# Encoder layer on one core: the feed-forwards in groups of four gate units, with seven block products in place of eight in two chunks of each eight

## The chip, the cores and the metric

The kernel runs on one core of one Trainium2 chip. The metric is device time in microseconds (us): 1980.3 us, the median of three runs of the kernel before (1979.99 to 1980.6).

## The reference, cut to what matters

One encoder layer over x[256, 2048] in float32. The two SwiGLU feed-forwards, which the change touches, hold most of the products; between them stands a mixer (one wide projection, a pooling branch, a convolution branch, an output projection).

```python
def rmsnorm(x, g):
    return x * rsqrt(mean(x * x) + EPS) * g
def swiglu(h, w_gate, w_up, w_down):          # w_gate, w_up: 2048 x 5632; w_down: 5632 x 2048
    return (silu(h @ w_gate) * (h @ w_up)) @ w_down

x = x + 0.5 * swiglu(rmsnorm(x, ffn1_norm), ffn1_w_gate, ffn1_w_up, ffn1_w_down)
x = x + mixer(rmsnorm(x, mix_norm))
x = x + 0.5 * swiglu(rmsnorm(x, ffn2_norm), ffn2_w_gate, ffn2_w_up, ffn2_w_down)
out = rmsnorm(x, final_norm)
```

## The kernel before, in words

**Products.** Every float32 operand is split into a high part (a cast to fp32r on ScalarE, ACT: `hi_lo`, line 135) and a low part (operand less high part on VectorE, DVE: line 137). A product is three matmuls: high by high, high by low, low by high (`products`, lines 203 to 214). The 256 tokens are two token tiles of 128; activations are the stationary operand (128 x 128), weights the moving one (128 x 512).

**The stream.** All weights pass through one stream of chunks. A chunk is two row tiles of 128 rows by 1024 columns, a tile of 512 KB each; a unit is all chunks of 1024 output columns. One ordinary chunk is 2 row tiles x 2 token tiles x 3 matmuls x 2 halves of 512 columns = 24 matmuls. A gate unit (512 columns of `w_gate` beside the same 512 of `w_up`) has 16 row tiles, so 8 chunks; each feed-forward has 11 gate units, then two down units (one for each half of the output) of 44 row tiles, so 22 chunks.

**The order.** It is written out by hand. For chunk i, `run` (lines 346 to 355) emits the loads of chunk i+2 on SP's queue, the split of chunk i+1 on ACT and DVE, then whatever `at` hung on chunk i, then the products of chunk i on TensorE (PE). Each engine goes through its own part in that order. Split tiles have four buffers for the high and four for the low parts (line 74), that is two chunks, so the split of a row tile of chunk i+1 waits until the matching row tile of chunk i-1 is used up; raw tiles have five buffers. In a unit's last chunk token tile 0 comes first, then token tile 1 (line 194).

**PSUM.** Accumulators are three buffers of two banks (line 77), so a unit starts while the last one is read out; two single banks serve transposes (line 78).

**After a gate unit** `gate_done` (lines 277 to 294) makes h = silu(gate) * up from the accumulators, for each token tile one ACT and one DVE instruction; two and three chunks later `put` turns h by PE transposes (line 250) and splits it into `ht`, which keeps all 11 units' hidden layer. The down units run after all gate units; `down_done` (lines 296 to 305) adds half their sum into the residual X and `squares` feeds the next norm. `next_operand` and `x_transposed` make the next transposed operand; for the first feed-forward `first_operand` makes it from `xT` during the first unit (lines 336 and 710).

Of the kernel before, what the change touches and what calls it, by code (L numbers as in the profile page):

```python
# [13 lines left out]
P = 128  # L14
# [21 lines left out]
# after these row tiles of weights, the row tiles of x^T that are loaded  # L36
# [4 lines left out]
# columns of the packed per-partition vectors  # L41
# [9 lines left out]
class Unit:  # L51
    """x[T, K*128] @ w[K*128, 1024]: K row tiles, two banks of 512 columns for each token tile."""

    def __init__(self, dram, k, lhs, done, tail=None):
        self.dram, self.k, self.lhs, self.done, self.tail = dram, k, lhs, done, tail
        self.acc = None


class Special:
    """A chunk of the weight stream with a use of its own."""  # L60
# [6 lines left out]
def encoder_kernel(ctx: ExitStack, tc: tile.TileContext, x, xT, vecs, rows, pool_m,  # L67
# [29 lines left out]
    def at(i, fn):  # L97
        """fn is emitted before the products of chunk i."""
        side.setdefault(i, []).append(fn)

    def amid(i, fn):
        """fn is emitted between the products of chunk i."""
        while isinstance(stream[i][0], Special):
            i += 1
        middle.setdefault(i, []).append(fn)

    class Pos:
        now = 0

# [10 lines left out]
    def load(i):  # L120
# [27 lines left out]
    def split_chunk(i, first=False):  # L148
# [3 lines left out]
        r = raw.pop(i)  # L152
        split[i] = []
# [11 lines left out]

    def bank(name):
        return ps_t.tile([P, C], F32, tag="T", name=name)

    def run_chunk(i):
# [33 lines left out]
    def products(u, k, t, w, cs=(0, 1)):  # L203
        xh, xl = u.lhs(k, t)
        wh, wl = w
        for n, (a, b) in enumerate(((xh, wh), (xh, wl), (xl, wh))):
            for c in cs:
# [4 lines left out]
                    start=k == 0 and n == 0,  # L212
                    stop=k == u.k - 1 and n == 2,
                )

    # ---------------------------------------------------------------- operands of the products
    def pair(pool, tag, n, name):
        """hi and lo by row tile, four row tiles to a block."""
# [9 lines left out]
    def hidden(pool, name):  # L228
        """The feed-forward's hidden layer, hi and lo by row tile, four of them in a block."""
        return [tuple(block(pool, f"h{s}{u}", F32R, f"{name}{s}{u}") for s in "hl") for u in range(FF // C)]  # L230
# [7 lines left out]
    def scaled_split(dst, src, gain):  # L238
        """dst = hi and lo of src * gain, a scalar of each partition."""
# [5 lines left out]
    def transposes(src_of, n, name):  # L245
        """n (up to 4 / NT) tiles [T, 128] into one bank as [128, T] each."""
        b = bank(name)
# [6 lines left out]
    def x_transposed(dst, gain_base, k0):  # L254
# [17 lines left out]
    # ---------------------------------------------------------------- feed-forward  # L272
    def ffn_units(w_g, w_d, xt, ht, rs, residual_done, tail=None):
        def hidden_lhs(k, t):
            return tuple(h[:, k % 4, t * P:(t + 1) * P] for h in ht[k // 4])

        def gate_done(u):
            def done(acc):
                hs = []
                for t in range(NT):  # L280
                    sg = stg.tile([P, C], F32, tag="sg", name=f"sg{Pos.now}_{t}")
                    h = stg.tile([P, C], F32, tag="h", name=f"h{Pos.now}_{t}")
# [4 lines left out]

                def put(k0):
                    b = transposes(lambda j, t: hs[t][:, (k0 + j) * P:(k0 + j + 1) * P], 2,
                                   f"hT{Pos.now}_{k0}")  # L290
                    hi_lo(b.rearrange("p (q t) -> p q t", q=2), *(h[:, k0:k0 + 2, :] for h in ht[u]))
                at(Pos.now + 2, lambda: put(0))
                at(Pos.now + 3, lambda: put(2))
            return done

        def down_done(half):
# [12 lines left out]
        for half in range(2):  # L309
# [517 lines left out]
```

## Time and profile before

| | before |
|---|---|
| runs | 1979.99, 1980.3, 1980.6 us |
| span of the profiled execution (first to last instruction) | 1978.6 us |
| instructions | 22916 |
| weights and other traffic read from HBM | 380.28 MB |

The profiled execution has no time of its own beside its span; the median of the runs lies 1.7 us above that span, which stands for what lies around it. PE is the matmuls, PEld the loads of the stationary operand that overlap them, DVE VectorE, ACT ScalarE, POOL GpSimd, SP the queue that issues the loads. The names in rows are those of the program: `acc` an accumulator, `wh` and `wl` the high and low weights, `xt1h` the high part of the first feed-forward's operand, `hT` the transposed hidden layer. A bracket behind a row gives the idle time before it and what ended it. Matmul durations overlap: the pace is read from their starts.

### The profile page before, as it was taken

The page shows a single profiled execution, that of the slowest core. Times are in us where ns is not written, and L with a number is a line of the kernel's source. Part 1 is how long each engine was busy: PE and PEld are TensorE (multiplying, and loading weights), DVE is VectorE, ACT ScalarE, POOL GpSimd, SP SyncE. Part 2 cuts the span into 40 slices and gives each one's busy share as a digit, 9 for nine tenths or more (in the row PEclk, how much of TensorE's full clock was granted, in tenths as well). Part 3 has the DMA queues.
Part 4 walks back from the last instruction along what each step waited for, and adds up shares of the span by engine and source line. Part 5 has one row for each costly group of instructions (what it writes and reads, how often), then busy time and mean ns, then how long its engine had stood idle before and what let it go on. Part 6 is the DMA issues. An engine that isn't in the chain of part 4 may idle for free.

```text
span 1978.6 us, 22916 instructions
## 1 busy us (share of the span) xinstructions
PE 1966.4 (99%) x8848; PEld 1629.5 (82%) x8848; DVE 1110.4 (56%) x1224; ACT 874.5 (44%) x997; POOL 11.0 (1%) x22
## 2 busy tenths in 40 slices
PE   9999999999999999999999999999999999999998
PEld 7888888888888888888888888888888888888886
DVE  5454544444445445888897765555544444444444
ACT  6444444444434345454444544544444444443433
POOL 0000000000000000000000000000000000000000
PEclk9999999999999999999999999999999999999999
DMA  8555555555555656666666555555555555565564
GB/s 310 193 188 196 190 192 188 187 189 190 192 191 187 195 189 202 194 195 211 202 208 205 184 185 185 181 186 198 191 188 189 189 190 192 181 198 195 192 192 149
DMA packets 106141, 383.88 MB, mean 194 GB/s; under 512 B 11920, under 2 KB 12176, under 8 KB 105776
## 3 DMA queue, kind: packets, MB, share of 16 engines
q1 hardware_dynamic: 104688, 378.45, 58.4%
q0 software_dynamic: 1056, 3.83, 0.6%
q8 instruction: 69, 1.13, 0.2%
q14 instruction: 40, 0.33, 0.1%
q10 hardware_dynamic: 288, 0.14, 0.0%
HBM read 380.28 MB, written 2.10 MB: 193 GB/s over the span
## 4 chain that ended last, share of the span: by engine, by line
PE 99%; DMA 1%; issue 0%; ACT 0%; DVE 0%; DVEq 0%; POOLq 0%; POOL 0%; ACTq 0%
PE acc L208 96%; PE hT L250 1%; PE xt L250 0%; DMA raw<-in_w_g 0%; PE mixb L560 0%; DMA xrh<-in_xT 0%; PE pool L535 0%; PE mT L250 0%; PE gT L250 0%; ACT fsq L668 0%; ACT wh L135 0%; PE ln_mean L442 0%; PE ln_var L471 0%; DVE X L680 0%; DVE X L665 0%
## 5 line engine op out<-in xcount | busy, mean ns | idle before, releaser
L137 DVE TENSOR_TENSOR wl<-raw,wh 128x1024 fp32r<-128x1024 f32 (+1 forms) x706 | 853.8, 1221 | 741.7 <-ACT wh L135 741.5
L135 ACT CAST wh<-raw 128x1024 fp32r<-128x1024 f32 (+1 forms) x706 | 736.2, 1050 | 906.9 <-PE acc L208 849.6
L208 PE MATMUL acc<-wh,xt1h 128*128 128x512 f32 x704 | 219.2, 392 | 1.8 <-ACT wh L135 0.9
L208 PE MATMUL acc<-wh,xt3h 128*128 128x512 f32 x704 | 218.9, 392 | 0.0
L208 PE MATMUL acc<-wl,xt1h 128*128 128x512 f32 x704 | 217.4, 390 | 0.1
L208 PE MATMUL acc<-wl,xt3h 128*128 128x512 f32 x704 | 217.1, 390 | 0.0
L208 PE MATMUL acc<-wh,xt1l 128*128 128x512 f32 x704 | 216.9, 389 | 0.0
L208 PE MATMUL acc<-wh,xt3l 128*128 128x512 f32 x704 | 216.8, 389 | 0.0
L208 PEld LDWEIGHTS acc<-wl,xt1h 128*128 128x128 f32 x704 | 132.1, 188 | 28.1 <-DVE wl L137 0.4
L208 PEld LDWEIGHTS acc<-wh,xt1l 128*128 128x128 f32 x704 | 132.1, 188 | 28.2 <-DVE xt1l L242 0.5
L208 PEld LDWEIGHTS acc<-wh,xt3l 128*128 128x128 f32 x704 | 132.1, 188 | 27.8
L208 PEld LDWEIGHTS acc<-wl,xt3h 128*128 128x128 f32 x704 | 132.1, 188 | 27.8
L208 PEld LDWEIGHTS acc<-wh,xt1h 128*128 128x128 f32 x704 | 130.6, 188 | 28.6 <-ACT wh L135 1.5
L208 PEld LDWEIGHTS acc<-wh,xt3h 128*128 128x128 f32 x704 | 130.5, 188 | 25.8
L208 PE MATMUL acc<-wh,xt2h 128*128 128x512 f32 x448 | 138.3, 390 | 0.0
L208 PE MATMUL acc<-wl,xt2h 128*128 128x512 f32 x448 | 138.1, 389 | 0.0
L208 PE MATMUL acc<-wh,xt2l 128*128 128x512 f32 x448 | 138.0, 389 | 0.0
L208 PE MATMUL acc<-wh,ht2h 128*128 128x512 f32 x352 | 109.2, 390 | 0.0
L208 PE MATMUL acc<-wl,ht2h 128*128 128x512 f32 x352 | 109.1, 389 | 0.0
L208 PE MATMUL acc<-wh,ht2l 128*128 128x512 f32 x352 | 109.0, 389 | 0.0
L208 PE MATMUL acc<-wh,ht1h 128*128 128x512 f32 x352 | 108.7, 390 | 0.0
L208 PE MATMUL acc<-wh,ht1l 128*128 128x512 f32 x352 | 108.4, 389 | 0.0
(144 smaller groups left out, 1699.9 us busy)
## 6 DMA issues: line engine op xcount, KB each, us to landing
raw<-in_w_g SPq DMA_DIRECT2D x350, 512.0 KB, 3.3
raw<-in_w_d SPq DMA_DIRECT2D x176, 512.0 KB, 3.5
raw<-in_w_in SPq DMA_DIRECT2D x112, 512.0 KB, 4.2
raw<-in_w_out SPq DMA_DIRECT2D x32, 512.0 KB, 4.2
raw<-in_w_pp SPq DMA_DIRECT2D x16, 512.0 KB, 4.0
raw<-in_w_cp SPq DMA_DIRECT2D x16, 512.0 KB, 4.0
row<-in_rows POOLq DMA_DIRECT2D x7, 512.0 KB, 4.2
X<-in_x SPq DMA_DIRECT2D x2, 1024.0 KB, 8.9
```

Source lines behind the costliest of these rows:

```text
L135: nc.scalar.copy(out=h, in_=src)
L137: nc.vector.tensor_tensor(out=l, in0=src, in1=h.bitcast(F32), op=ALU.subtract)
L208: nc.tensor.matmul(u.acc[t + c if u.tail and t else t][:, c, :], lhsT=a, rhs=b[:, c * C:(c + 1) * C], start=k == 0 and n == 0, stop=k == u ...
L250: nc.tensor.transpose(out=b[:, j * T + t * P: j * T + (t + 1) * P], in_=src_of(j, t), identity=ident)
```

## The change

- **Order.** The gate units come in groups of four: after gate units 0 to 4 come the two down units of the hidden rows of gate units 0 to 3 (8 chunks each), after gate units 5 to 8 those of gate units 4 to 7, after 9 and 10 those of the last three (6 chunks each). Each down unit adds into X; only the last two feed the norm. `ht` holds four gate units' hidden layer in place of eleven.
- **Seven products.** In chunks 0 and 3 of every gate unit but the first, and of the down units of the first two groups, the two row tiles and the two column halves of the weights, and the two row tiles and two token tiles of the activations, are taken as 2 x 2 blocks, and seven block products (Strassen's scheme in Winograd's form) replace eight. Three of them add into the unit's own accumulators, four into shared banks that serve several outputs.
- **Sums of weights.** `split_seven` makes four sums of 128 x 512 on DVE, one of them in place in the raw tile, and splits three more column blocks of 512 into high and low parts.
- **Differences of activations.** `e_forms` makes four of 128 x 128 on DVE and splits them: once a feed-forward for the operand's chunks 0 and 3 (`scaled_forms`), and for chunks 0 and 3 of every group's hidden layer in `put`, that is, for gate units 0, 4 and 8 in its first call and 1, 5 and 9 in its second.
- **Shared banks.** After chunk 3 `shared_parts` combines the four banks into two tiles in SBUF (one ACT copy, four DVE instructions). At the end the own accumulators are added to these (`gate_done_seven`), or both go into X one after the other (`into_residual`).
- **PSUM** is one tile of eight banks: four shared, four own, without a second set. `put` of a gate unit's hidden layer now runs in chunks 5 and 6 of the following gate unit, in two of the shared banks.

```diff
+GROUP = 4
+SEVEN = (0, 3)
+B_P1, B_P5, B_P6, B_P7, B_11, B_12, B_21, B_22 = range(8)
...
-    ps_a = ctx.enter_context(tc.tile_pool(name="ps_a", bufs=3, space=bass.MemoryType.PSUM))
-    ps_t = ctx.enter_context(tc.tile_pool(name="ps_t", bufs=2, space=bass.MemoryType.PSUM))
+    psp = ctx.enter_context(tc.tile_pool(name="psp", bufs=1, space=bass.MemoryType.PSUM))
+    ps = psp.tile([P, 8, C], F32, name="ps")
...
-                nc.sync.dma_start(out=r[:, s], in_=u.dram[2 * cc + kk, :, s])
+                nc.sync.dma_start(out=r[:, s], in_=u.dram[getattr(u, "k0", 0) + 2 * cc + kk, :, s])
...
+        if isinstance(u, Unit) and cc in u.seven:
+            split[i] = split_seven(i, *r)
+            return
...
+    def split_seven(i, r0, r1):
+        w11, w12, w21, w22 = r0[:, :C], r0[:, C:], r1[:, :C], r1[:, C:]
+        sm = ffn["pool"].tile([P, 3, C], F32, tag="sum", name=f"sum{i}")
+
+        def add(out, a, b):
+            nc.vector.tensor_tensor(out=out, in0=a, in1=b, op=ALU.add)
+        add(sm[:, 1, :], w12, w22)
+        add(w12, w11, w12)
+        add(sm[:, 0, :], w12, w22)
+        add(sm[:, 2, :], sm[:, 0, :], w21)
+        ext = tuple(ffn["pool"].tile([P, 3, C], F32R, tag=f"ext{x}", name=f"ext{x}{i}") for x in "hl")
+        return (hi_lo(r0, *stream_tiles(i, 0)), hi_lo(sm, *ext), hi_lo(r1, *stream_tiles(i, 1)))
...
     def bank(name):
-        return ps_t.tile([P, C], F32, tag="T", name=name)
+        Pos.bank += 1
+        return ps[:, 6 + Pos.bank % 2, :]
...
         if cc == 0:
             n = NT + 1 if u.tail else NT
-            u.acc = [ps_a.tile([P, 2, C], F32, tag="acc", name=f"acc{i}_{t}") for t in range(n)]
+            if u.seven:
+                u.acc = [ps[:, B_11:B_12 + 1, :], ps[:, B_21:B_22 + 1, :]]
+                Pos.acc = 0
+            else:
+                u.acc = [ps[:, 2 * ((Pos.acc + t) % 3):2 * ((Pos.acc + t) % 3) + 2, :] for t in range(n)]
+                Pos.acc += n
+            if u.start:
+                u.start()
         ws = split.pop(i)
+        if cc in u.seven:
+            products_of_seven(u, cc, ws)
+            if cc == u.seven[-1]:
+                at(i + 1, u.early)
+            return
...
-                    start=k == 0 and n == 0,
+                    start=(t, c) not in u.begun,
...
+    def products_of_seven(u, cc, ws):
+        f = u.forms(cc)
+        (eh, el), (sh, sl), (oh, ol) = ws
+        left, right = slice(0, C), slice(C, W2)
+        shared = [(B_P1, "A11", eh[:, left], el[:, left]), (B_P5, "E5", eh[:, right], el[:, right]),
+                  (B_P6, "E6", sh[:, 0, :], sl[:, 0, :]), (B_P7, "E7", sh[:, 1, :], sl[:, 1, :])]
+        own = [(B_21, "A22", sh[:, 2, :], sl[:, 2, :]), (B_11, "A12", oh[:, left], ol[:, left]),
+               (B_12, "E3", oh[:, right], ol[:, right])]
+        for b, form, wh, wl in own + shared if u.start else shared + own:
+            xh, xl = f[form]
+            where = divmod(b - B_11, 2) if b >= B_11 else b
+            for n, (x_, w_) in enumerate(((xh, wh), (xh, wl), (xl, wh))):
+                nc.tensor.matmul(ps[:, b, :], lhsT=x_, rhs=w_, start=where not in u.begun,
+                                 stop=b < B_11 and cc == u.seven[-1] and n == 2)
+                u.begun.add(where)
...
+    def e_forms(dst, even, odd):
+        e = stg.tile([P, 4, P], F32, tag="sg", name=f"e{Pos.now}")
+        a11, a21, a12, a22 = even[:, :P], even[:, P:], odd[:, :P], odd[:, P:]
+        for n, (a, b) in enumerate(((a11, a21), (a21, a22), (a11, e[:, 1, :]), (a12, e[:, 2, :]))):
+            nc.vector.tensor_tensor(out=e[:, n, :], in0=a, in1=b, op=ALU.subtract)
+        hi_lo(e, *dst)
...
+    def scaled_forms(dst, src, gain_base, k0):
+        y = stg.tile([P, 2, T], F32, tag="sg", name=f"y{Pos.now}_{k0}")
+        for j in range(2):
+            nc.scalar.activation(y[:, j, :], src[j], AF.Copy, scale=vcol(gain_base, k0 + j))
+        e_forms(dst, y[:, 0, :], y[:, 1, :])
...
+        if es and k0 // 2 in es:
+            scaled_forms(es[k0 // 2], [b[:, j * T:(j + 1) * T] for j in range(2)], gain_base, k0)
...
+        def put(u, hs, k0, b=None):
+            b = transposes(lambda j, t: hs[t][:, (k0 + j) * P:(k0 + j + 1) * P], 2, f"hT{Pos.now}_{k0}", b)
+            hi_lo(b.rearrange("p (q t) -> p q t", q=2), *(h[:, k0:k0 + 2, :] for h in ffn["ht"][u % GROUP]))
+            c = (u % GROUP) * 2 + k0 // 2
+            if c in SEVEN:
+                y = stg.tile([P, 2, T], F32, tag="sg", name=f"hy{Pos.now}_{k0}")
+                nc.scalar.copy(out=y, in_=b.rearrange("p (q t) -> p q t", q=2))
+                e_forms(ffn["hE"][c], y[:, 0, :], y[:, 1, :])
...
+        def gate_done_seven(u):
+            def done(acc):
+                hs = []
+                for t in range(NT):
+                    z = ffn[f"t{t}"]
+                    nc.vector.tensor_tensor(out=z, in0=acc[t], in1=z, op=ALU.add)
+                    nc.scalar.activation(z[:, 0, :], z[:, 0, :], AF.Silu, scale=rs[:, t:t + 1])
+                for t in range(NT):
+                    z = ffn[f"t{t}"]
+                    h = hidden_tile(t)
+                    nc.vector.scalar_tensor_tensor(out=h, in0=z[:, 1, :], scalar=rs[:, t:t + 1],
+                                                   in1=z[:, 0, :], op0=ALU.mult, op1=ALU.mult)
+                    hs.append(h)
+                waiting.append((u, hs))
+            return done
+        def shared_parts():
+            z0, z1 = ffn["t0"], ffn["t1"]
+            nc.scalar.copy(out=z0[:, 0, :], in_=ps[:, B_P1, :])
+            for out, a, b, op in ((z1[:, 1, :], ps[:, B_P6, :], z0[:, 0, :], ALU.subtract),
+                                  (z0[:, 1, :], ps[:, B_P5, :], z1[:, 1, :], ALU.add),
+                                  (z1[:, 0, :], ps[:, B_P7, :], z1[:, 1, :], ALU.subtract),
+                                  (z1[:, 1, :], z0[:, 1, :], ps[:, B_P7, :], ALU.subtract)):
+                nc.vector.tensor_tensor(out=out, in0=a, in1=b, op=op)
+
+        def gate_early():
+            shared_parts()
+            if waiting:
+                u, hs = waiting.pop()
+                at(Pos.now + 1, lambda: put(u, hs, 0, ps[:, B_P6, :]))
+                at(Pos.now + 2, lambda: put(u, hs, 2, ps[:, B_P1, :]))
+
+        def into_residual(t, half, part):
+            xs = X[t][:, half * W2:(half + 1) * W2]
+            nc.vector.scalar_tensor_tensor(out=xs, in0=part.rearrange("p a b -> p (a b)"), scalar=0.5, in1=xs,
+                                           op0=ALU.mult, op1=ALU.add)
+
+        def down_early(half):
+            def early():
+                shared_parts()
+                for t in range(NT):
+                    at(Pos.now + 1 + t, lambda t=t: into_residual(t, half, ffn[f"t{t}"]))
+            return early
...
+        def down_done(half, last):
             def done(acc):
                 for t in range(NT):
-                    for c in range(2):
-                        xs = X[t][:, half * W2 + c * C: half * W2 + (c + 1) * C]
-                        nc.vector.scalar_tensor_tensor(out=xs, in0=acc[t][:, c, :], scalar=0.5, in1=xs,
-                                                       op0=ALU.mult, op1=ALU.add)
-                    squares(t, 2 * half, half * W2, (half + 1) * W2)
-                residual_done(half)
+                    into_residual(t, half, acc[t])
+                    if last:
+                        squares(t, 2 * half, half * W2, (half + 1) * W2)
+                if last:
+                    residual_done(half)
             return done
...
-        for u in range(FF // C):
-            add_unit(Unit(w_g[u], KD, lhs_of(xt), gate_done(u)))
-        for half in range(2):
-            add_unit(Unit(w_d[half], KF, hidden_lhs, down_done(half), tail if half else None))
+        def rest_of_hidden():
+            u, hs = waiting.pop()
+            at(Pos.now + 2, lambda: put(u, hs, 0))
+            at(Pos.now + 3, lambda: put(u, hs, 2))
...
+        units = FF // C
+        for u in range(units):
+            if u:
+                add_unit(Unit(w_g[u], KD, lhs_of(xt), gate_done_seven(u), forms=forms_of(lhs_of(xt), xE),
+                              early=gate_early, seven=SEVEN, start=(lambda: None) if u == 1 else None))
+            else:
+                add_unit(Unit(w_g[u], KD, lhs_of(xt), gate_done(u)))
+            if u and u % GROUP == 0:
+                add_down(u // GROUP - 1, 4 * GROUP, False)
+        add_down((units - 1) // GROUP, 4 * (units - (units - 1) // GROUP * GROUP), True)
...
-            next_operand(xt3, V_N2, rstd[2])(half)
+            next_operand(xt3, V_N2, rstd[2], xE3)(half)
...
-    at(KD // 2, lambda: ht1.extend(hidden(htp, "ht1")))
+    for c in SEVEN:
+        at(c + 3, lambda c=c: scaled_forms(xE1[c], [xr[c // 2][:, 2 * c % 4 + j, :] for j in range(2)], V_N1, 2 * c))
```

## Rows read from the trace of the kernel before

**Rows 1.** The page's parts 1 and 2: busy time by engine, granted clock in 40 slices.

```profile
PE 1966.4 (99%) x8848; PEld 1629.5 (82%) x8848; DVE 1110.4 (56%) x1224; ACT 874.5 (44%) x997; POOL 11.0 (1%) x22
...
PEclk9999999999999999999999999999999999999999
```

**Rows 2.** Chain that ended last, in order of time: start us, us, what.

```profile
286.32 38.10 PE acc L208 x168
...
330.80 38.10 PE acc L208 x168
```

**Rows 3.** Waits, all engines: who waited for whom, us in total, times, longest.

```profile
ACT wh L135 <- PE acc L208: 849.6, 520, 3.0
DVE wl L137 <- ACT wh L135: 741.5, 549, 3.6
...
ACT xt2h L241 <- DVE xt2l L242: 7.8, 8, 1.6
```

**Rows 4.** Stretches: busy of PE, PEld, DVE, ACT, POOL; clock; DMA; GB/s; last row one unit.

```profile
14.70:499.20 484.50, 484.50 (x2175) 401.09 (x2176) 245.53 (x232) 217.27 (x247) 1.38 (x2) 1.00 0.59 198
...
741.50:1241.30 499.80, 499.80 (x2288) 416.14 (x2287) 378.69 (x541) 238.00 (x289) 5.04 (x7) 1.00 0.61 196
...
sum 44.50, PE 44.50 PEld 36.84 DVE 22.16 ACT 19.00 POOL 0.00; mean PE 5.56 PEld 4.61 DVE 2.77 ACT 2.37 POOL 0.00
```

**Rows 5.** Timeline of the last chunk, by columns: start, us, engine, instruction.

```profile
1963.82 0.39 PE L208 MATMUL acc<-wh,ht2h 128*128 128x512 f32 x1
...
1964.04 0.39 PE L208 MATMUL acc<-wl,ht2h 128*128 128x512 f32 x1
```

**Rows 6.** Groups by line and shape: busy us, mean ns of one, idle before.

```profile
L137 DVE TENSOR_TENSOR wl<-raw,wh 128x1024 fp32r<-128x1024 f32 x702 | 851.2, 1224 | 741.7 <-ACT wh L135 741.5
L135 ACT CAST wh<-raw 128x1024 fp32r<-128x1024 f32 x702 | 734.0, 1053 | 906.9 <-PE acc L208 849.6 <-DVE conv L419 25.2 <-ACT wh L135 7.2
...
L284 DVE SCALAR_TENSOR_TENSOR h<-acc,rstd,sg 128x512 f32<-128x512 f32 x44 | 33.0, 751 | 68.3 <-ACT sg L283 68.3
L283 ACT ACTIVATE sg<-acc,rstd 128x512 f32<-128x512 f32 x44 | 30.4, 690 | 78.4 <-PE acc L208 78.3
...
L137 DVE TENSOR_TENSOR ht1l<-hT,ht1h 128x512 fp32r<-128x512 f32 x22 | 15.0, 683 | 0.0
...
L135 ACT CAST ht1h<-hT 128x512 fp32r<-128x512 f32 x22 | 12.8, 581 | 0.0
...
L581 DVE SCALAR_TENSOR_TENSOR gate<-acc,rstd,row 128x1024 f32<-128x1024 f32 x8 | 10.2, 1280 | 2.3 <-PE acc L208 2.3
...
L594 DVE TENSOR_TENSOR gate<-acc,gate 128x1024 f32<-128x1024 f32 x4 | 4.8, 1219 | 0.7 <-PE acc L208 0.7
...
L481 DVE TENSOR_SCALAR ln_diag<-ident,ln_r 128x128 f32<-128x128 f32 x2 | 0.5, 281 | 0.0
```

**Rows 7.** Timeline, a gate unit's third chunk and the next unit's start.

```profile
285.83 0.49 PE L250 MATMUL hT<-ident,h 128*128 128x128 f32 x3
285.92 1.05 ACT L135 CAST wh<-raw 128x1024 fp32r<-128x1024 f32 x1 [1.67 <-PE acc L208]
...
287.00 1.23 DVE L137 TENSOR_TENSOR wl<-raw,wh 128x1024 fp32r<-128x1024 f32 x1 [1.49 <-ACT wh L135]
...
289.10 1.05 ACT L135 CAST wh<-raw 128x1024 fp32r<-128x1024 f32 x1 [1.65 <-PE acc L208]
...
320.68 3.50 DVE L137 TENSOR_TENSOR wl<-raw,wh 128x1024 fp32r<-128x1024 f32 x3 [0.19 <-ACT wh L135]
```

**Rows 8.** Timeline, ACT, DVE and PE at the end of the first gate unit.

```profile
44.43 0.91 ACT L241 ACTIVATE xt1h<-xrl,vec 128x256 fp32r<-128x256 f32 x2
...
46.68 2.37 DVE L137 TENSOR_TENSOR wl<-raw,wh 128x1024 fp32r<-128x1024 f32 x2
...
49.52 1.28 ACT L283 ACT_TABLE_LOAD   x1 [1.73 <-PE acc L208]
...
51.98 0.61 PE L208 MATMUL acc<-wh,xt1h 128*128 128x512 f32 x2
```

More of the change, by code (lines that the diff above doesn't have):

```diff
@@ L51, with __init__ @@
 class Unit:
-    def __init__(self, dram, k, lhs, done, tail=None):
+    def __init__(self, dram, k, lhs, done, tail=None, k0=0, forms=None, early=None, start=None, seven=()):
         self.dram, self.k, self.lhs, self.done, self.tail = dram, k, lhs, done, tail
+        self.k0, self.forms, self.early, self.start, self.seven = k0, forms, early, start, seven
         self.acc = None
+        self.begun = set()
 class Special:
@@ L108, in encoder_kernel @@
         now = 0
+        acc = 0
+        bank = 0
     def add_unit(u):
@@ L228, in hidden, with e_tiles, forms_of, f @@
     def hidden(pool, name):
-        return [tuple(block(pool, f"h{s}{u}", F32R, f"{name}{s}{u}") for s in "hl") for u in range(FF // C)]
+        return [tuple(block(pool, f"h{s}{u}", F32R, f"{name}{s}{u}") for s in "hl") for u in range(GROUP)]
+    def e_tiles(pool, tag, n):
+        return {c: tuple(pool.tile([P, 4, P], F32R, tag=f"{tag}E{x}{c}", name=f"{tag}E{x}{c}_{n}") for x in "hl")
+                for c in SEVEN}
+    def e_forms(dst, even, odd):
[4 more added lines that the diff above has]
+        hi_lo(e, *dst)
+    def forms_of(lhs, es):
+        def f(c):
+            eh, el = es[c]
+            r = {n: (eh[:, q, :], el[:, q, :]) for q, n in enumerate(("E7", "E5", "E6", "E3"))}
+            r.update(A11=lhs(2 * c, 0), A12=lhs(2 * c + 1, 0), A22=lhs(2 * c + 1, 1))
+            return r
+        return f
+    def scaled_forms(dst, src, gain_base, k0):
[3 more added lines that the diff above has]
+        e_forms(dst, y[:, 0, :], y[:, 1, :])
     def lhs_of(pairs):
@@ L243, in scaled_split, with transposes @@
                                        op0=ALU.mult, op1=ALU.subtract)
-    def transposes(src_of, n, name):
-        b = bank(name)
+    def transposes(src_of, n, name, b=None):
+        b = bank(name) if b is None else b
         for j in range(n):
@@ L270, in finish_rstd, with open_ffn, ffn_units, hidden_tile @@
         nc.gpsimd.tensor_tensor(dst, msq, mhalf, op=ALU.pow)
-    def ffn_units(w_g, w_d, xt, ht, rs, residual_done, tail=None):
-        def hidden_lhs(k, t):
-            return tuple(h[:, k % 4, t * P:(t + 1) * P] for h in ht[k // 4])
+    ffn = {}
+    def open_ffn(stack, n):
+        pool = ffn["pool"] = stack.enter_context(tc.tile_pool(name=f"ffn{n}", bufs=1))
+        ffn["ht"] = hidden(pool, f"ht{n}")
+        ffn["hE"] = e_tiles(pool, "h", n)
+        ffn["t0"], ffn["t1"] = (pool.tile([P, 2, C], F32, tag=f"part{t}", name=f"part{n}_{t}") for t in range(NT))
+    def ffn_units(w_g, w_d, xt, xE, rs, residual_done, tail=None):
+        waiting = []
+        def hidden_lhs(k, t):
+            return tuple(h[:, k % 4, t * P:(t + 1) * P] for h in ffn["ht"][k // 4])
+        def put(u, hs, k0, b=None):
[6 more added lines that the diff above has]
+                e_forms(ffn["hE"][c], y[:, 0, :], y[:, 1, :])
+        def hidden_tile(t):
+            return stg.tile([P, C], F32, tag="h", name=f"h{Pos.now}_{t}")
         def gate_done(u):
@@ L286, in done @@
                     hs.append(h)
[L288 to L293, printed above, removed]
-            return done
-        def down_done(half):
+                waiting.append((u, hs))
@@ new lines, in done, with add_down @@
+                if last:
+                    residual_done(half)
+            return done
+        def rest_of_hidden():
+            u, hs = waiting.pop()
+            at(Pos.now + 2, lambda: put(u, hs, 0))
+            at(Pos.now + 3, lambda: put(u, hs, 2))
+        def add_down(g, k, last):
+            for half in range(2):
+                if last:
+                    add_unit(Unit(w_d[half], k, hidden_lhs, down_done(half, True), tail if half else None,
+                                  k0=g * GROUP * 4, start=None if half else rest_of_hidden))
+                else:
+                    add_unit(Unit(w_d[half], k, hidden_lhs, down_done(half, False), k0=g * GROUP * 4,
+                                  forms=forms_of(hidden_lhs, LateE()), early=down_early(half), seven=SEVEN))
@@ L323, in encoder_kernel @@
     xt1 = pair(xtp, "x", KD, "xt1")
+    xE1 = e_tiles(xtp, "x", 1)
     def start():
@@ L624, in encoder_kernel @@
     xt3 = []
+    xE3 = {}
     def wo_done(half):
@@ L653, in encoder_kernel @@
     n2 = len(stream)
-    ht2 = []
     fin = {}
@@ L696, in encoder_kernel @@
     at(n3 - 1, final_first_half)
-    xr = [block(htp, f"h{s}{FF // C - 1 - j}", F32, f"xr{s}{j}") for j in range(2) for s in "hl"]
+    xr = [block(ffn["pool"], f"xr{j}", F32, f"xr{j}") for j in range(4)]
     start()
@@ L733, in encoder_kernel @@
     ht_stack = ExitStack()
-    htp = ht_stack.enter_context(tc.tile_pool(name="ht2", bufs=1))
-    ht2.extend(hidden(htp, "ht2"))
+    open_ffn(ht_stack, 2)
     run(n2, n3)
```

22 lines of the change are left out of this document (14 added, 8 removed).

## Prediction

> **What bounds the kernel now.** I read the page first: PE is busy for 1966.4 of 1978.6 us, DVE for 56% and ACT for 44%, and the granted clock is full in all 40 slices [rows 1]. The chain in order of time shows what PE's time is made of: a piece of 168 matmuls takes 38.10 us, and one such piece starts 44.48 us after the last [rows 2]. So a matmul of 512 columns costs 38.10 / 168 = 0.2268 us, an ordinary chunk of 24 costs 5.44 us, and a gate unit's 192 matmuls and 8 transposes cost 44.5. The waits point one way: ACT waits for PE (849.6 us) to hand back split buffers, DVE waits for ACT (741.5), and PE waits for neither to any amount [rows 3]. The stretches agree: in the first feed-forward's gate units DVE works 245.53 of 484.50 us, in the mixer 378.69 of 499.80, with PE filled in both [rows 4]. PE is the bound; fewer matmuls shorten the kernel as long as DVE keeps up, and a DVE at 76% did not hold it up.
>
> **What is removed.** A chunk of seven has 7 x 3 = 21 matmuls, not 24. In each feed-forward 10 gate units and 4 down units have two such chunks: 14 x 2 x 3 = 84 matmuls, 168 in both. Their successors differ in two things, a new stationary operand for every matmul and three matmuls in a row into one bank. The last chunk before has the second already, and its matmuls start 0.22 us apart (1963.82, 1964.04) [rows 5]; I therefore price them all alike: 168 x 0.2268 = **38.1 us** gone. The Trainium skill (TensorE: Matmul & The Clock Gate, section "Wait — 56ns, not 53.3ns?") gives 215.7 ns between such matmuls; by that estimate it would be 36.2 us, but the pace of the trace decides.
>
> **What is added at no cost on PE.** Bytes loaded are the same and SP's order only changes rows; the transposes are as many as before. In the last group's down units, everything is as it was at the end of a down unit, with the end of the kernel (tail, norm, stores) unchanged.
>
> **What is added on DVE and ACT.** Prices [rows 6]: a DVE instruction on 1024 columns 1.22, on 512 0.68, on 128 0.28 us; one of 1536 is in no row, and lies between 1.22 + (1.22 - 0.68) = 1.76 (the slope) and 1.22 + 0.68 = 1.90 (two instructions); I take 1.76, since it is one instruction. A cast costs 1.05 for 1024, 0.58 for 512, and by the same slope 1.52 for 1536. A chunk of seven so costs DVE 4 x 0.68 + 2 x 1.22 + 1.76 = 6.9 us in place of 2.4. A seven-unit on DVE: six ordinary chunks 14.7, two of seven 13.9, `shared_parts` 2.7, the two sums at the end 2.4, h 1.5, `put` 1.4: 36.6 us, with the differences up to 38.4, of the 43.1 us that the unit then lasts (44.5 - 6 x 0.2268). Before it was 22.16 of 44.50 [rows 4]. DVE goes to 85 to 89%, ACT to some 55%. On average both are hidden under PE; what counts is whether DVE's order lets a bank go too late, since the own banks have no second set.
>
> **The boundary between two units**, walked in time from the start of chunk 6, PE in chunks of 5.44. A row tile's cast starts as PE gives its buffer back (285.92, 289.10) and DVE follows 1.1 later [rows 7]. So chunk 7's second low part is done at 2.4, `put`'s low part at 3.0. The four weight sums, which need only raw tiles, then run to 5.6, the first low part to 6.7, the 1536 one (its cast needs all four sums) to 8.9, the second to 10.0. Successive DVE instructions of 1024 start 1.14 apart (three in 3.50) [rows 7], so these are slightly late rather than early. The sum for token tile 0 ends at 11.2; that for tile 1 waits for chunk 7's last matmul at 11.3 (0.43 for transposes, 2 x 5.44) and ends at 12.6. PE begins the next unit with the four shared products, 12 x 0.2268 = 2.7 us, and wants bank 6 at 14.0: 1.4 us to spare. Behind a down unit `into_residual` (1.22 to 1.28) stands in place of `put`: about 0.9 to spare. I take both as hidden; the cover is those 12 matmuls, and without it each boundary would cost 2.7 - 1.4 = 1.3 us.
>
> **Where the cover is too short: differences in chunk 6.** The second `put` of gate units 1, 5 and 9 falls into chunk 6 of units 2, 6 and 10 and makes them. ACT's copy of the same bank has to wait for DVE's low part, as the trace shows of two readers of one bank (xt2h waits for xt2l, 7.8 us in 8 times) [rows 3]. The Trainium skill (PSUM — Partial Sum Buffer, section "PSUM bank collisions raise a hardware error") says that ScalarE and VectorE must not even read one bank at the same time, and that rule costs here; without it the copy would start earlier and the four stalls below be some 0.9 us shorter each, 1948 us in all, an estimate. Walk: low part 3.0, copy 3.6, four differences 4.6, cast 5.2, low part 5.9, sums 8.5, low parts 9.6, 11.8 and 12.9, token sums 14.1 and 15.2. Bank 6 is wanted at 14.0: PE stalls 1.2 us. Silu, h, and the casts of the next chunk come as much later, and its first low part is missing for another 0.5. That is 1.7 us at the ends of units 2 and 6 (after unit 10 comes a down unit that starts in free banks): 4 x 1.7 = **6.8 us**. Bounds: 0 (the 1.4 of spare covers more) to 3.4 each.
>
> **The first unit.** `scaled_forms` in chunk 6 stands behind ACT's squares and `first_operand` (44.43 to 45.3) and ahead of the first split of seven, on which DVE before began at 46.68 [rows 8]. Now the differences and their parts end at 49.0, the sums at 51.6, the low parts at 52.7, 54.9 and 56.1. PE wants the 1536 columns' high part at 51.98 [rows 8], as unit 1 starts with its own banks, and gets it at 53.2, the low one at 54.9, the next at 56.1: 1.1 + 1.5 + 0.4 = **3.0 us** (0 to 4). The second feed-forward has its differences earlier, in chunks 2 and 3 of the mixer's last unit: for each 2 x 0.5 + 0.58 = 1.6 us of ACT and 4 x 0.28 + 0.68 = 1.8 of DVE, beside 5.44 of PE; hidden, else 0 to 1.
>
> **Sum.** 38.1 - 6.8 - 3.0 = 28.3 us. The span goes from 1978.6 to 1950.3; the runs lie 1.7 above it, so **1952.0 us**. Bounds: nothing stalls, 1942.2; all stalls at their upper ends (13.6 + 4 + 1) and the other 22 boundaries 0.4 over, 1980.3 - 38.1 + 18.6 + 8.8 = 1969.6.
>
> **Rivals.**
> - *No stall at all* (0.25). DVE's starts at 1.14 for 1.22 give back a few tenths at each step, and PE, if it falls behind once, stays behind where DVE wants it. Against it: 1.2 us is more than those tenths. 1942.2 us.
> - *DVE late at every boundary* (0.16). The spare of 0.9 to 1.4 us rests on five hand-overs between ACT and DVE, and on PSUM reads (1.22 for 1024 columns [rows 6]) that never ran at so full a DVE in a row. With 1 us of stall at each of the 26 boundaries between seven-units and 3.0 at the start: 1980.3 - 38.1 + 26 + 3 = 1971 us. For: DVE at 85 to 89% is above the mixer's 76%. From 38.1 / 26 = 1.5 us at each, nothing is gained.
> - *Waits by tile, not by bank* (0.07): slower. The eight banks are one tile; before, an accumulator of two banks was one. Were the program's waits set by tile, PE could not go on in any bank while another is read: in chunk 4 until `shared_parts` ends (2.4 + 4 x 0.68 = 5.1), in chunks 5 and 6 until the transposes' low parts (3.0 each), at the end two sums (2.4). That is 13.5 us for each of 20 gate units and 5.1 + 2.6 = 7.7 for each of 8 down units: 1980.3 - 38.1 + 270 + 62 = 2274 us. It decides from a wait of 6 x 0.2268 = 1.4 us in a unit. For it no row speaks; against it, that a wait by bank is all that reads of separate banks need.
>
> The forecast has 0.52. The change does what it says: 21 matmuls for 24 can be counted in its code, and the pace inside one bank has its row.
>
> **Range and chances.** 1941 to 1972 takes in the forecast, the case without stalls and the late DVE up to 1 us a boundary. 0.2%, 4 us, is about what a measurement of this kernel can tell from no change. Faster by more: 0.52 + 0.25 + 0.09 of the late DVE = 0.86; within: 0.05 (DVE 1.3 to 1.5 us late); slower: 0.07 + 0.02 = 0.09.
>
> **What would show it.** Right: 168 fewer matmuls at 0.2268, DVE near 85% in gate units, and PE's idle time before the own banks' first matmul, put down to the sums of `gate_done_seven`, only at the ends of units 2 and 6 and to weights' parts at the start of unit 1. Wrong: idle time of PE at every unit's start (the late DVE), in chunks 4 to 6 (waits by tile), or matmuls of seven at another pace.

## The result, and the profile after

The changed kernel takes **1959.75 us** (median of four runs, 1958.93 to 1960.31) against 1980.31 for the kernel before on the same chip: a ratio of 0.9896, 95% interval 0.9882 to 0.991. That is 20.6 us saved, where 28.3 were forecast and 38.1 left PE. The profiled run, the fastest of the four, took 1958.93 us, so the median lies 0.8 above it; what follows in this section is read from that run. Two runs of the experiments below, one of the groups alone (2470.75 us) and one with chunks 0 and 2 (2422.11 us), had a granted clock of 0.75 and are left out of the times given.

The page's parts 1 (busy time), 2 (DVE's busy share in 40 equal slices, in tenths) and 4 (the chain that ended last, shares by engine) of the changed kernel answer to [rows 1]:

```profile
span 1957.1 us, 23246 instructions
...
PE 1933.4 (99%) x8680; PEld 1598.3 (82%) x8680; DVE 1521.7 (78%) x1762; ACT 979.2 (50%) x1117; POOL 11.0 (1%) x22
...
DVE  6888888888888655888898766588887888888865
...
PE 94%; DVE 3%; ACT 1%; issue 1%; DMA 1%; DVEq 0%; POOLq 0%; ACTq 0%; POOL 0%
```

168 matmuls are gone (8848 to 8680), PE still fills 99% of the span, and DVE has risen from 1110.4 to 1521.7 us. The chain that ended last shows both kinds of chunk, and answers to [rows 2] (start us, us, what):

```profile
115.80 4.76 PE ps L277 x21
120.56 5.44 PE ps L256 x24
```

21 matmuls in 4.76 us are 0.2267 us each: the same pace as in an ordinary chunk. The waits of PE answer to [rows 3], where PE waited for nothing to speak of (us in total, times, longest):

```profile
PE ps L277 <- DVE part L413: 6.6, 4, 1.7
PE ps L343 <- DVE xt3l L335: 1.7, 1, 1.7
PE ps L277 <- ACT exth L153: 1.4, 1, 1.4
PE ps L277 <- DVE extl L155: 1.3, 1, 1.3
```

Three places, then: the sums of `gate_done_seven` (`part`, L413) four times, the transposes of the mixer's last unit (L343) once, and the first split of seven (`exth`, `extl`) once. Everywhere else the new work is covered, though DVE is far fuller than in [rows 4]. This is one stretch of gate units (the columns of rows 4):

```profile
170.00:240.00 70.00, 70.00 (x318) 57.92 (x318) 57.90 (x60) 35.10 (x37) 0.00 (x0) 1.00 0.55 183
```

PE is busy for all 70 us, DVE for 57.90, 83%. The new operations answer to the prices of [rows 6]:

```profile
L155 DVE TENSOR_TENSOR extl<-sum,exth 128x1536 fp32r<-128x1536 f32 x56 | 98.5, 1759 | 22.9 <-ACT exth L153 22.9
...
L153 ACT CAST exth<-sum 128x1536 fp32r<-128x1536 f32 x56 | 83.1, 1484 | 14.8 <-DVE sum L193 14.8
```

**Where the 38.1 us went.** I take the distance between the starts of successive matmuls; what it has above 0.227 us is time that PE lost. Counting distances over 0.33, the kernel before lost 3.8 us and this one 19.9: 16.1 more. They are 4 x 2.37 = 9.5 at four boundaries, 5.3 at the start of unit 1, 1.7 in the mixer, and 0.5 less than before in the first chunks. 38.1 - 16.1 = 22.0; the last matmul starts 21.6 us earlier than before.

**A boundary that stalls**, the end of unit 2 of the first feed-forward. DVE's timeline (start us, us, engine, line, operation, out and in):

```profile
134.24 0.68 DVE L155 TENSOR_TENSOR ht1l<-ps,ht1h 128x512 fp32r<-128x512 f32 x1
135.58 0.49 DVE L307 TENSOR_TENSOR e<-hy 128x128 f32<-128x128 f32 x2 [0.65 <-ACT hy L389]
...
137.41 0.69 DVE L155 TENSOR_TENSOR hEl<-e,hEh 128x512 fp32r<-128x512 f32 x1 [0.69 <-ACT hEh L153]
138.02 0.68 DVE L193 TENSOR_TENSOR sum<-raw,raw 128x512 f32<-128x512 f32 x1
138.74 0.69 DVE L193 TENSOR_TENSOR raw<-raw 128x512 f32<-128x512 f32 x1
...
142.44 1.76 DVE L155 TENSOR_TENSOR extl<-sum,exth 128x1536 fp32r<-128x1536 f32 x1 [0.41 <-ACT exth L153]
144.11 1.22 DVE L155 TENSOR_TENSOR wl<-raw,wh 128x1024 fp32r<-128x1024 f32 x1
145.25 2.35 DVE L413 TENSOR_TENSOR part<-ps,part 128x1024 f32<-128x1024 f32 x2
```

And PE's:

```profile
145.61 0.39 PE L277 MATMUL ps<-exth,xEl 128*128 128x512 f32 x1
147.65 0.50 PE L277 MATMUL ps<-exth,xt1h 128*128 128x512 f32 x1 [1.66 <-DVE part L413]
...
150.61 0.74 PE L256 MATMUL ps<-wl,xt1h 128*128 128x512 f32 x2 [0.17 <-DVE wl L155]
```

The last of the twelve shared matmuls starts at 145.61; the thirteenth needs bank 6 and starts 2.04 us later, as the second sum ends (145.25 + 2.35 = 147.60).

### The profile page after: what moved, and what is told of

The parts are those of the page before. It is cut to its first block, busy times and chain, and to the rows that moved or that the text cites. A ratio compares the mean times of both kernels' runs of the same rounds, so it can differ in the third digit from the quotient of the medians.

```text
span 1957.1 us, 23246 instructions
## 1 busy us (share of the span) xinstructions
PE 1933.4 (99%) x8680; PEld 1598.3 (82%) x8680; DVE 1521.7 (78%) x1762; ACT 979.2 (50%) x1117; POOL 11.0 (1%) x22
## 4 chain that ended last, share of the span: by engine, by line
PE 94%; DVE 3%; ACT 1%; issue 1%; DMA 1%; DVEq 0%; POOLq 0%; ACTq 0%; POOL 0%
PE ps L256 78%; PE ps L277 13%; PE ps L343 1%; DVE wl L155 1%; DVE sum L193 1%; DVE part L413 0%; DVE extl L155 0%; ACT exth L153 0%; ACT wh L153 0%; DVE e L307 0%; DMA raw<-in_w_g 0%; PE ps L740 0%; ACT sq L358 0%; DMA xr<-in_xT 0%; PE ps L715 0%
## 5 line engine op out<-in xcount | busy, mean ns | idle before, releaser
L256 PE MATMUL ps<-wh,xt1h 128*128 128x512 f32 x544 | 169.9, 393 | 1.3 <-ACT wh L153 1.0
L256 PE MATMUL ps<-wh,xt3h 128*128 128x512 f32 x544 | 169.6, 393 | 0.0
L256 PE MATMUL ps<-wl,xt1h 128*128 128x512 f32 x544 | 168.3, 390 | 0.4 <-DVE wl L155 0.3
L256 PE MATMUL ps<-wl,xt3h 128*128 128x512 f32 x544 | 168.1, 390 | 0.3 <-DVE wl L155 0.3
L256 PE MATMUL ps<-wh,xt1l 128*128 128x512 f32 x544 | 167.7, 389 | 0.1
L256 PE MATMUL ps<-wh,xt3l 128*128 128x512 f32 x544 | 167.6, 389 | 0.0
L256 PE MATMUL ps<-wh,xt2h 128*128 128x512 f32 x448 | 138.5, 390 | 0.0
L256 PE MATMUL ps<-wh,xt2l 128*128 128x512 f32 x448 | 138.0, 389 | 0.0
L256 PE MATMUL ps<-wl,xt2h 128*128 128x512 f32 x448 | 137.9, 389 | 0.0
L256 PEld LDWEIGHTS ps<-wh,xt3l 128*128 128x128 f32 x544 | 102.1, 188 | 21.7
```

The costliest lines, as they stand in the source:

```text
L256: nc.tensor.matmul(u.acc[t + c if u.tail and t else t][:, c, :], lhsT=a, rhs=b[:, c * C:(c + 1) * C], start=(t, c) not in u.begun, stop=k ...
```

## The experiments

All ratios are to the kernel before, run on the same chip; the changed kernel without an edit has 0.9896.

**The groups alone.** Every unit is ordinary again; what is left is the order in groups of four, the part sums and one PSUM tile of eight banks.

```diff
-SEVEN = (0, 3)
+SEVEN = ()
...
-add_unit(Unit(w_g[u], KD, lhs_of(xt), gate_done_seven(u), ..., seven=SEVEN, ...))
+add_unit(Unit(w_g[u], KD, lhs_of(xt), gate_done(u), start=rest_of_hidden if u else None))
```

> The groups of four alone: no chunk takes seven products, no weight sums, no differences; the down units still come in groups and each gate unit's hidden layer is put in chunks 2 and 3 of the next gate unit. Same function. Theory A (the groups cost nothing, and the whole effect is that of the seven products and what they bring): 8848 matmuls, 1980.3 us within 1 us (1979 to 1982). Rival B (the more frequent changes between gate and down units, four more additions into the residual, cost PE time of their own, hidden so far in the balance): 1983 to 1990.

1980.63 us, 1.0001 (0.9991 to 1.0011). Groups and the single tile cost nothing that these runs can tell from zero (the interval is 2 us to either side); waits go by bank, since PE loses no more behind the start-up than in the kernel before, and the change comes from the chunks of seven.

**One chunk of seven in each unit, not two.**

```diff
-SEVEN = (0, 3)
+SEVEN = (0,)
```

> Chunk 0 alone takes seven products; half the products are saved, same function. Theory A (PE is the bound and each matmul left out gives its 0.2268 us): 84 matmuls, 19.05 us, less a stall of some 1 us at the start of unit 1 and the 1.7 in the mixer's last unit; no differences ahead of a boundary: 1980.4 - 19.05 + 2.8 = 1964.2 us (1962.5 to 1966). Rival B (a chunk of seven costs PE more than its 21 matmuls, by the changes of bank and operand): 0.3 us for each of 28 chunks, 1972 or more.

1964.73 us, 0.992 (0.9903 to 0.9938). Half the matmuls are saved, and the four boundaries do not stall: the second `put` makes no differences. 84 matmuls are 19.0 us; unit 1 loses 1.3 and the mixer 1.7, which leaves 16.0, and 15.8 were saved. So the changes of bank and operand cost PE nothing that shows, against B.

**The differences out of chunk 6**, by hanging those of the second `put` on chunk 1 of the next unit.

```diff
-                y = stg.tile([P, 2, T], F32, tag="sg", ...)
+                y = ffn["pool"].tile([P, 2, T], F32, tag="y", ...)
-                e_forms(ffn["hE"][c], y[:, 0, :], y[:, 1, :])
+                if k0: at(Pos.now + 3, lambda: e_forms(ffn["hE"][c], y[:, 0, :], y[:, 1, :]))
+                else: e_forms(ffn["hE"][c], y[:, 0, :], y[:, 1, :])
```

> The differences of the second put's hidden tiles move from chunk 6 to chunk 1 of the following unit; nothing is left out, and the computation is the same. Theory A (the four stalls at the ends of units 2 and 6 come from these differences standing ahead of the weight sums in DVE's order): the four pairs of gaps between matmul starts (1.8 and 0.3 us over the pace, with 0.1 more after each) vanish, 4 x 2.4 = 9.5 us: 1959.8 - 9.5 = 1950.3 us (1949 to 1952). Rival B (DVE is full over the whole unit, so that the moved work only stalls PE elsewhere, in chunks 2 to 4 or at the next boundary): less than 3 us gained, 1957 to 1960.

1949.51 us, 0.9845 (0.9828 to 0.9861). The waits of PE no longer name `part`; all four gaps are gone, 9.5 us by their distances, and 10.2 us of the median with them. So it was the differences' place, not their cost, that stalled PE: DVE has as much to do as before (57.84 us in the stretch of 70 us above).

**The copy ahead of the low part** in `put`: ACT reads the bank for the differences before DVE does.

```diff
+                nc.scalar.copy(out=y, in_=bq)
             nc.vector.tensor_tensor(out=lo, in0=bq, in1=hi.bitcast(F32), op=ALU.subtract)
-                nc.scalar.copy(out=y, in_=bq)
```

> In the changed kernel ACT's copy for the differences is emitted ahead of DVE's low part of the same bank. Same computation. Theory A (the copy that has to wait for DVE's reading of the same bank is 0.6 us of each of the four stalls): the chain to the weight sums gets 0.6 us shorter, the gaps of 2.04 us shrink to 1.4, 4 x 0.6 = 2.4 us gained, 1957.4 us (1956 to 1958.5). Rival B (the copy is hidden behind DVE's own queue): gaps as they were, 1959.8.

1956.2 us, 0.9875 (0.9859 to 0.9891). The distance at the four boundaries goes from 2.04 to 1.29 us. In the changed kernel ACT stood idle until DVE's low part ended at 134.92, and its copy started 0.04 us later:

```profile
134.96 0.59 ACT L389 COPY hy<-ps 128x512 f32<-128x512 f32 x1 [1.41 <-DVE ht1l L155]
```

With the copy first the two change places, still without meeting, and DVE's differences start 0.60 us behind the low part's start in place of 1.34:

```profile
133.82 0.59 ACT L391 COPY hy<-ps 128x512 f32<-128x512 f32 x1
...
134.61 0.68 DVE L392 TENSOR_TENSOR ht1l<-ps,ht1h 128x512 fp32r<-128x512 f32 x1
135.21 0.48 DVE L307 TENSOR_TENSOR e<-hy 128x128 f32<-128x128 f32 x2
```

**The first unit's differences two chunks earlier**, ahead of the squares instead of behind them.

```diff
-        at(c + 3, lambda c=c: scaled_forms(xE1[c], ...))
+        at(4 if c else 3, lambda c=c: scaled_forms(xE1[c], ...))
```

> In the first feed-forward's first unit the differences of the operand's chunk 3 are made in chunk 4, ahead of ACT's squares, in place of chunk 6. Same computation. Theory A (unit 1 starts late because these differences stand ahead of its first split, and the stall then lets the clock fall): DVE's sums begin some 2.4 us earlier, the stall of 3.7 us shrinks to 1 to 1.5, the granted clock stays full from 50 to 64 us and the eight matmuls at 0.43 us go: 2.4 + 1.6 = 4 us gained, 1955.8 us (1954.5 to 1957). Rival B (the split of seven itself is what is late there, 6.9 us of DVE in one chunk with the table load on ACT behind it): the stall stays above 3 us and less than 1 us is gained.

1955.92 us, 0.9876 (0.9862 to 0.9891). The first split of seven is on time with its casts; one wait of 1.18 us for `extl` stays, and the clock holds (below). By the distances unit 1 loses 1.9 us at its start in place of 5.3. The time lies in A's range.

**No cover**: every chunk of seven, and so every unit of seven, starts with its own banks.

```diff
-        for b, form, wh, wl in own + shared if u.start else shared + own:
+        for b, form, wh, wl in own + shared:
```

> Every chunk of seven begins with the products into the own banks. Same computation. Theory A (the 12 matmuls into shared banks, 2.7 us, are what covers the reading of the own banks): PE then waits at each of the 26 boundaries between units of seven until DVE's second sum is done, which in the changed kernel ended 1.42, 1.73, 2.25 or 4.48 us after the unit's start (8, 6, 8 and 4 times): 11.4 + 10.4 + 18 + 17.9 - 7.3 (already lost at the four) = 50 us more, and 0.1 to 0.2 at each restart: 1959.8 + 54 = 2014 us (2005 to 2025), slower than the kernel before. Rival B (the order of the banks does not matter, since PE's own pipeline or the banks' readers hide it): 1958 to 1965.

2027.42 us, 1.0237 (1.0222 to 1.0253): slower than the kernel before. The direction is theory A's, the size is 13 us more, just outside its range. The waits of PE in this kernel:

```profile
PE ps L277 <- DVE part L413: 39.4, 18, 4.5
PE ps L277 <- DVE X L443: 17.9, 8, 2.2
```

All 26 boundaries now wait, 57.3 us in sum. By the distances of starts an ordinary one loses 1.57 us (8 times), one whose chunk 5 has differences 1.88 (6 times), one behind a down unit 2.40 (8 times), and each of the four stalls of before 4.63, 61.6 us in all where the change lost 7.3. That is 54.3 of the 66.7 us lost more. Most of the other 12, which theory A did not have, are matmuls at the lower clock: it fell behind those four and behind two of the eight gaps at down units (last section).

**All three moves**: differences of the hidden layer late, of the first unit early, and those of the second feed-forward's operand hung two chunks behind `x_transposed`, not between its two transposes.

```diff
-        y = stg.tile([P, 2, T], F32, tag="sg", ...)
+        y = stg.tile([P, 2, T], F32, tag="sg" if gain_base == V_N1 else "h", ...)
         for j in range(2):
             nc.scalar.activation(y[:, j, :], src[j], AF.Copy, scale=vcol(gain_base, k0 + j))
-        e_forms(dst, y[:, 0, :], y[:, 1, :])
+        if gain_base == V_N1: e_forms(dst, y[:, 0, :], y[:, 1, :])
+        else: at(Pos.now + 2, lambda: e_forms(dst, y[:, 0, :], y[:, 1, :]))
...
```

(The other two moves are edited as above.)

> Three moves together: the second put's differences in chunk 1 of the following unit, the first unit's differences in chunk 4, and in the mixer's last unit the scaled copies taken from the bank at once but the differences two chunks later. Same computation. Theory A (the three waits are separate, each worth what its gaps measured): 1949.5 - 3.9 (the second alone) - 1.7 (one gap of 1.95 between transposes at 1196.24) = 1943.9 us (1942.5 to 1945.5), within 2 us of the 1942.2 without any stall. Rival B (taking one wait away uncovers the next, since DVE is full): 1946.5 to 1949.5.

**1944.27 us**, 0.9816 (0.9799 to 0.9834), faster than both kernels. Of the 16.1 us only 1.9 are left behind the start-up, at the start of unit 1. Of the 38.1 us of matmuls saved some 36 are now won.

**Chunks 0 and 2 in place of 0 and 3**, everything else as in the change.

```diff
-SEVEN = (0, 3)
+SEVEN = (0, 2)
```

> The changed kernel with chunks 0 and 2 in place of 0 and 3; as many products, sums and differences, the same function. All hidden tiles with differences then fall into the first put, now in chunk 4, and none stands ahead of the next unit's first split. Theory A (it is the place of the differences that stalls, not their number): the four stalls go (9.5), the first unit's differences are made in chunk 5 ahead of the squares (some 3.9), and the gap in the mixer's last unit stays: 1959.8 - 13.4 = 1946.4 us (1945 to 1949). Rival B (two chunks of seven two apart come too soon for DVE): PE waits for low parts in chunk 2 of 28 units, 0.5 to 1 us each, 1960 to 1975.

1952.01 us, 0.9856 (0.9838 to 0.9874), between the two theories. The four boundaries do not stall, as A says. But the first unit now makes its second differences in chunk 5, together with the squares, and PE waits 1.4 us there for `xt1h`; units 0 and 1 lose 5.3 us together, the mixer 1.7. And in 18 units a matmul of the second chunk of seven starts 0.06 us late, for `extl`: 1.2 us more.

**A third chunk of seven** in each gate unit, on top of all three moves. The down units take chunks 0 and 2 (`SEVEN_H`).

```diff
-SEVEN = (0, 3)
+SEVEN = (0, 2, 4)
+SEVEN_H = (0, 2)
...
-                if k0: at(Pos.now + 3, ...)
-                else: e_forms(...)
+                at(Pos.now + 4, lambda: e_forms(ffn["hE"][c], y[:, 0, :], y[:, 1, :]))
...
-        at(4 if c else 3, lambda c=c: scaled_forms(xE1[c], ...))
+        at(3 + c // 2, lambda c=c: scaled_forms(xE1[c], ...))
```

> Kernel: as the one with all three moves, and the gate units have a third chunk of seven: chunks 0, 2 and 4 in place of 0 and 3; the down units of seven have chunks 0 and 2, and differences of the hidden layer are made four chunks after put. 20 gate units x 3 matmuls x 0.2268 = 13.6 us less on PE than with all three moves (1944.3), that is 1930.7. DVE gets 4.5 us more in a gate unit (6.9 for 2.4) and goes from 83% to some 95% of the unit's 42.4 us.
> Theory A (DVE costs PE time only where its order lets a bank go too late, not by its share): walked as in the prediction the second sum of a boundary now ends at 13.1 plus the measured 0.6, wanted at 14.0, so 0.3 us to spare at each boundary and 1931, between 1930 and 1937 with some boundaries a few tenths late.
> Theory B (at such a share DVE is the bound, and falls behind by what it lacks in each unit): 1 us or more at each of 20 gate units gives back 20 us or more, 1951 and up, with PE's gaps at chunks of seven all over the feed-forwards.

1954.88 us, 0.987 (0.9854 to 0.9887). 60 more matmuls are gone, and it is 10.6 us slower than with two chunks: the time is in B's range. But the gaps are not all over the feed-forwards, as B has it: ten gate units lose 1.74 us each at chunk 4, those in whose chunk 2 the differences are made; the start of the first feed-forward takes most of the rest. Two whole units side by side (columns of rows 4), from the first matmul of one to that of the next, the first without differences, the second with:

```profile
189.16:231.67 42.51, 42.51 (x192) 35.05 (x191) 39.25 (x42) 23.17 (x24) 0.00 (x0) 1.00 0.61 199
144.84:189.16 44.32, 43.13 (x193) 34.90 (x191) 41.02 (x47) 23.76 (x25) 0.00 (x0) 1.00 0.57 190
```

With 39.25 us of DVE's work in a unit of 42.51 PE does not lose anything; with 41.02, which would be 96% of those 42.51, the unit takes 1.8 us more. DVE's busy share does not tell the two apart, 92 and 93%, since the wait stretches the unit.

**The same with the differences behind the third split**, in chunk 4, and the first unit's in chunks 2, 3 and 4.

```diff
-                at(Pos.now + 4, lambda: e_forms(...))
+                at(Pos.now + 6, lambda: e_forms(...))
-        at(3 + c // 2, lambda c=c: scaled_forms(xE1[c], ...))
+        at(2 + c // 2, lambda c=c: scaled_forms(xE1[c], ...))
```

> Kernel: as the one with three chunks of seven, and only the differences are moved: those of the hidden layer six chunks after put in place of four, that is to chunk 4, behind the last of the three weight splits; those of the first unit's operand to chunks 2, 3 and 4 in place of 3, 4 and 5, ahead of the squares. With three chunks PE waited at chunk 4 in 10 gate units alone, 1.73 us in each, those whose chunk 2 makes the differences, and 5.5 us in units 0 and 1; a gate unit without differences ran without a wait with DVE busy 39.26 of 42.50 us.
> Theory A (order, not share): from the start of a unit to chunk 4 PE gives 20.4 us and the splits and h take 20.2, so 1.8 us of differences there are late, and behind that split they have room. 17.3 us of waits and most of the 5.5 go: 1933, between 1931 and 1937.
> Theory B (share: DVE has 39.3 + 1.8 = 41 of 42.4 us in such a unit, and the lag only moves to the next place): the ten units wait 1 us or more elsewhere, 1944 and up.

1945.49 us, 0.9823 (0.981 to 0.9836): 9.4 us better, 12 short of A and in B's range. The wait at chunk 4 is gone, but the lag moves to the next unit, as B says, in eight places:

```profile
141.28 0.50 PE L278 MATMUL ps<-wh,xt1h 128*128 128x512 f32 x1 [0.43 <-DVE ht1l L156]
153.81 0.50 PE L278 MATMUL ps<-extl,xEh 128*128 128x512 f32 x1 [0.38 <-DVE extl L156]
```

Each loses 1.4 us at these two matmuls together, once for a bank that `put`'s low part still reads and once for `extl`. So with three chunks DVE had too little left for another 1.8 us at either of the two places tried, and the third chunk gave nothing over the version with two. Whether a better order exists with three was not tried further.

## Why the prediction was right, and where it missed

The time lies in the range and the mechanism was the one forecast; three terms of the sum were too small. The range, 1941 to 1972, also holds two of the rivals, so the time alone, 7.8 us above the forecast, decides little between them: the places of PE's waits do.

- *What is removed*: 168 matmuls at 0.2267, forecast 0.2268. 38.1 us is right; the Trainium skill's 215.7 ns (TensorE: Matmul & The Clock Gate, section "Wait — 56ns, not 53.3ns?") was not the pace here.
- *What is added on DVE and ACT*: 1.759 us for the 1536 columns (1.76 taken), 1.484 for the cast (1.52), DVE 83% (85 to 89), ACT 50% (55). The prices are right, the shares came out a little lower, and DVE at 83% did not delay PE by its share.
- *The boundary between two units*: no gap at 22 of 26. The second sum ends 1.42 us behind the unit's start where 2.72 are to be had, so 1.3 to spare against 1.4; behind a down unit 0.5, against 0.9. The cover's price without it was forecast at 1.3 for each boundary; without it an ordinary one lost 1.57, and one behind a down unit 2.40, against 2.7 - 0.9 = 1.8.
- *Differences in chunk 6*: the place and the mechanism are right, shown by their move. The **size was off**: 2.37 us each, not 1.7. The timeline above tells where. Set its first low part's end, 134.92, to the walk's 3.0: then the differences and their parts end at 6.2 (walk 5.9), the sums at 9.0 (8.5: four dependent instructions start 0.72 apart, though one takes 0.69), the low parts at 13.4 (12.9), the second sum at 15.7 (15.2). Every hand-over was a little later than the durations add up to, and PE, which wanted the bank at 13.9, stalled 1.8 in place of 1.2. What follows behind the restart was 0.55, against 0.5.
- *ACT's copy waits for DVE's low part*: with the copy first the four stalls were 0.75 us shorter each, near the 0.9 estimated. The Trainium skill (PSUM — Partial Sum Buffer, section "PSUM bank collisions raise a hardware error") says that two engines must not access one bank at the same time. The trace agrees: ACT idles for 1.41 us and starts 0.04 us after DVE's low part ends. The other order does not test it, because DVE's low part, 0.20 us behind the copy's end, came straight behind the weights' low part on DVE's queue.
- *The first unit*: the walk was right to 0.1 us (`exth` 53.11, walk 53.2; `extl` 54.91, walk 54.9; the last part 56.04, walk 56.1). PE came there earlier than in the trace of before, so it waited 3.7 in place of 3.0 us, at no loss. What the term lacked was the clock: 1.6 us for eight matmuls at half speed.
- *The mixer's last unit*: "hidden, else 0 to 1" was **wrong**: 1.73 us. I set DVE's 1.8 us against a chunk of PE, but PE's own transposes need the two spare banks. DVE's timeline there, and PE's next transposes:

```profile
1194.03 0.66 DVE L307 TENSOR_TENSOR e<-y 128x128 f32<-128x128 f32 x2 [0.54 <-ACT y L322]
...
1196.02 0.69 DVE L155 TENSOR_TENSOR xEl<-e,xEh 128x512 fp32r<-128x512 f32 x1 [0.69 <-ACT xEh L153]
1196.63 0.48 DVE L335 SCALAR_TENSOR_TENSOR xt3l<-ps,vec,xt3h 128x256 fp32r<-128x256 f32 x1
1197.65 0.48 DVE L335 SCALAR_TENSOR_TENSOR xt3l<-ps,vec,xt3h 128x256 fp32r<-128x256 f32 x1 [0.54 <-ACT xt3h L334]
```

```profile
1198.20 0.66 PE L343 MATMUL ps<-ident,X 128*128 128x128 f32 x4 [1.68 <-DVE xt3l L335]
```

  The differences stand on DVE's queue ahead of the second pair's low parts, which free the bank. With the differences two chunks later this gap is gone.

The misses are 4 x 0.67 = 2.7, 5.3 - 3.0 = 2.3 and 1.7, together 6.7 us. The span came out at 1957.1, 6.8 above the forecast; the 0.5 gained in the first chunks are balanced by 0.4 of gaps below 0.1 us.

**The rivals.** *No stall at all* was put at 1942.2; with the three moves the kernel comes to 1944.27, within two microseconds of it, but not with the order of the change. *DVE late at every boundary* did not come with two chunks of seven; a third brings waits where differences are made. *Waits by tile* is out: the groups alone, with the same single tile, took 1980.63 us, 0.2 more than the kernel before on the same chip.

## What to carry to other kernels

An engine beside the bottleneck costs time by where its queue stands when a buffer must come free, and hardly by its share: 83% cost 16 us in one order and 2 in another, with the same work. So walk each deadline (a bank, an operand) and ask what is queued ahead of the instruction that meets it; let the unit that begins start in buffers that were freed early, and hang work without a deadline behind the next one. When that engine's work in a unit nears the unit's own length (41.0 of 42.5 us here), moving work, in the two ways tried, only moved the wait.

## What was not expected of the hardware

The clock of TensorE fell behind the long waits at the start of unit 1. Stretches of the changed kernel (columns of rows 4; the granted clock is the figure behind POOL's):

```profile
52.00:56.00 4.00, 1.46 (x4) 0.67 (x4) 3.58 (x3) 3.97 (x5) 0.00 (x0) 1.00 0.39 131
56.00:60.00 4.00, 3.96 (x10) 3.13 (x11) 3.86 (x5) 3.41 (x5) 0.00 (x0) 0.57 0.49 145
60.00:100.00 40.00, 40.00 (x181) 33.07 (x180) 31.58 (x36) 18.93 (x20) 0.00 (x0) 1.00 0.59 196
```

After a stretch in which PE worked 1.46 of 4 us, eight matmuls started 0.427 us apart, not 0.227: the lower level, 1.2 GHz, for 3.4 us. With the early differences PE worked 2.65 us of the same stretch, and the next one kept the full clock:

```profile
52.00:56.00 4.00, 2.65 (x11) 1.58 (x10) 3.95 (x4) 3.97 (x5) 0.00 (x0) 1.00 0.49 144
56.00:60.00 4.00, 4.00 (x19) 3.29 (x19) 3.90 (x5) 3.12 (x4) 0.00 (x0) 1.00 0.68 229
```

Without the cover it fell again behind a 4.85 us gap:

```profile
145.00:150.50 5.50, 1.57 (x7) 0.96 (x6) 5.09 (x5) 2.35 (x3) 0.00 (x0) 0.98 0.43 137
150.50:156.00 5.50, 4.96 (x12) 3.97 (x13) 4.16 (x5) 3.32 (x5) 0.00 (x0) 0.50 0.34 118
```

Behind the single gaps of 2.04 us of the changed kernel it did not fall. In the kernel without the cover it fell behind all four gaps of 4.85 us, behind none of the fourteen of 1.8 to 2.1, and behind two of the eight of 2.63, as here at 559.39 (seven matmuls at 0.427 us, granted clock 0.79 over the stretch):

```profile
559.00:566.50 7.50, 5.25 (x17) 3.93 (x16) 5.42 (x6) 2.65 (x3) 0.00 (x0) 0.79 0.52 158
```

So a gap of one length can cost that length alone or more; the two waits at the start of unit 1 cost 1.6 us on top of 3.7.
